# A two-layer hybrid encoder step on one core: bias rows copied in DRAM in three parts, planner costs and stage biases changed

## The chip, the core and the metric

The program runs on one core of a Trainium2 chip. The metric is device microseconds of one execution. The engines are TensorE (PE; its weight loads are shown as PEld), VectorE (DVE), ScalarE (ACT), GpSimdE (POOL) and SyncE (SP). Each runs its own instruction list in order and waits on semaphores for the others. All DMAs of this kernel are issued from SP's list.

## The reference

One inference step of two layers over 576 tokens: 512 prompt tokens and 64 sample tokens with 1024 cached keys. Each layer normalizes x and projects it, and three mixers read the projection:

```python
z = rmsnorm(x, norm_g) @ w_in                  # 1024 -> all columns of A, B, C and the gates
# A: differential attention, 4 heads, two softmax maps per head, T5 bias
bias = bias_a[t5_bucket(k_pos[None, :] - q_pos[:, None])]
logits = q k^T / 8 + bias;  a = p[:, :, 0] - lam * p[:, :, 1];  o = a v
# B: an indexer scores the keys, the top k (128 prompt, 256 sample) are kept, 8 heads attend to them
score = sum_h wi_h * relu(qi_h ki^T);  idx = top_k(score);  logits = q k_sel^T / 8 + bias_b
# C: chunked retention, 4 heads, decay, rotary
y = x + (sum_n sigmoid(gate_n) * ((o_n * silu(g_n)) @ w_branch[n])) @ w_out
```

The T5 bias depends on the distance of key and query alone, for 12 heads (4 of A, 8 of B). Outputs are y, the new keys and values, and the retention states, for prompt and sample.

## The kernel before, in words

Tokens lie in five tiles: t = 0 to 3 of 128 prompt tokens, t = 4 of 64 sample tokens. Every large product is made of three fp32r products of a high and a low part: the weights come by DMA into `wraw` (two buffers), ACT casts them to `whi`, DVE subtracts to `wlo` (two buffers), and PE multiplies hi·hi, lo·hi, hi·lo (`proj_tok`, L622, with tokens in the rows; `proj_ch`, L634, with channels in the rows). `x_norm` (L541 to L565) loads x, normalizes it (DVE, POOL for the power) and transposes it on PE (L562) into `xh` and `xl`.

`wload_idx` and `idx_proj` (L508 to L513, L748 to L755) make the indexer's product first; from it come the keys of B, written out (L737) and transposed by PE (L690). `keys_T` (L669, L670) loads cached keys with four DMAs and transposes them on DVE. `idx_prompt` and `idx_sample` score the keys (L789 to L797), and `topk` finds the largest by rounds of MAX8 and MATCH_REPLACE8 on DVE (L829, L830): 16 rounds for each of three prompt tiles and 32 for the sample, in each layer.

The bias: `build_windows` (L424 to L436, step `w0`) multiplies `rel_bias` by a table of one-hot columns on PE (L431), copies the result to SBUF (L433), writes 12 rows of 352 numbers to `gdram` in DRAM (L435), and copies each row 128 times within DRAM into `grep` (L436; 2112 KB). `dwin` (L438) and `dwin_s` then read skewed windows out of `grep` (L441, L449), into four buffers `D` and one `Ds`, and DVE overwrites a corner of each (L442).

The order of the instructions is not that of the code. A step list (`STEPS`) names the stages (x, i, iq, cv, gc, ...), each with two numbers, one for each layer, its bias in priority. `Order.plan` lists all instructions, gives each a cost (`_cost`), plays the five queues forward in time, and whenever an engine is free takes the ready instruction with the smallest priority (place in the program plus bias). `pin` then ties each engine's instructions into that order. A change of a cost or a bias therefore moves instructions on every engine, and never what they compute.

Of the kernel before, what the change touches and what calls it, by code (L numbers as in the profile page):

```python
# [12 lines left out]
F32 = mybir.dt.float32  # L13
# [74 lines left out]
        "sg": 2, "o": 2, "z": 4, "D": 4, "Ds": 1, "ss": 13, "ssn": 4, "nm": 7, "Z": 3, "sso": 2, "m8": 11, "z3": 1,  # L88
        "zz": 7, "qs": 1, "zk": 1, "qks": 3, "qd": 1}
STEPS = """  # L90
pw0+-2700/-3200 x0+0/-3900 x1+-11000/0 x2+3500/1700 x3+3900 w0+300/-5700 x4+-7800/0 i0+9200/4200 iq0+9300/5200
cv0+9700/1000 i1+-20100/-32500 gc1+-5800/1600 cq0+-800/14000 gc0+15200/18400 ca0+700 cv1+20500/-1900
sc0+3400/4900 cq1+-5100/900 ca1+-3800/-4000 kc0+4200/-400 ak0+2000/1900 i2+-18000/-17000 top2+30200/7600
ga0+0/-4400 sc1+-900 aq0+9200/-800 av0+400/3200 mc3+1200/8900 mc2+11900/-4200 top3+300/13700 aa1+2900/-5300
aa0+1500/-4000 mc0+24100/-3300 vc0+6000/5400 ak1+1400/-100 mc1+-1300/-2800 aq1+-13900/8000 av1+10300/10100
ga1+-8100/-6800 sa0+500/2600 aa3+-5200/-9000 gb0+-500/-6500 top1+0/6200 aa2+-16000/-18400 gb1 top4+30600/28400
kc1+-5500/-9000 bq0+4700/1500 sa1+-5800/-2400 bp0+-5900 ma1+10900/10500 bs0+-19100/-19900 ma0+11500/-2900
bq1+-400/0 bp1 sb0+-4800/-3100 ma3 ma2+5900/5600 bs1+1000/0 sb1+-2300/-5100 mb1+6200 mb0+-1200/-5200 mb2+0/-100
mb3
"""  # L100
PB = {"pj": 3, "s": 2, "t": 3}

# [1 line left out]
class Order:  # L104
# [44 lines left out]
    def _area(self, o):  # L149
# [17 lines left out]
            m = r  # L167
        return t.name, p0, p0 + o.ap[0][1], m << off

    def _cost(self, i, e, ins, outs):  # L170
        cols = self._cols
        n = max(cols(o) for o in ins[:1] + outs[:1]) if ins else cols(outs[0])
        if e == "SP":
            for o in outs[:1]:
                n = cols(o) * o.ap[0][1]
            return n / 90.0
        if e == "PE":
            n = cols(outs[0])
            if outs[0].bass_ap.tensor.name in self.psum and outs[0].bass_ap.offset >= 64 * 512:
                return 94.0  # L180
            if "float32r" in str(ins[0].dtype):
                return max(n * 0.4375 + 7, 112.0)
            if i.is_transpose:
                return 110.0
            return 2 * max(n / 1.2 + 5, 112.0)
        ps = any(o.bass_ap.tensor.name in self.psum for o in ins)
        if e == "Activation":
            return (51 if ps else 94) + n / 1.2 + 93 * (len(outs) - 1) + 93 * (len(ins) > 1)
        if e == "Pool":
            return 300 + 164 * n if "pow" in str(getattr(i, "op", "")) else 145 + n * 2.12  # L190
        op = str(i.opcode)
        if op == "Memset":
            return 40 + n * 0.26
        wide = [o for o in ins if cols(o) > 1]
        fast = not ps and len(wide) == 1 and op in ("TensorCopy", "TensorScalarPtr")
        ptr = op in ("TensorScalarPtr", "ISA") and len(ins) > len(wide) and n > 4
        return 68 + n * (0.52 if fast else 1.042) + 61 * ptr
# [48 lines left out]
    def plan(self):  # L246
        ops, users = self._graph()
        n = len(ops)
# [47 lines left out]
        for _ in range(n):  # L296
# [14 lines left out]
            order[e].append(k)  # L311
            start[k] = t
            if e == "SP":
                clock[e] = t + 475
                dma = max(dma, t + 1100) + cost
                end[k] = dma + 750
            else:
                if e == "PE":
                    if shared != rows:
                        cost += 90 if shared else 190  # L320
                        rows = shared
                    idle = max(0.0, idle + max(0.0, t - clock[e]) - (t - seen) * 0.35)
                    seen = t
                    if idle > 1300 and clock[e] > 0:
                        slow, idle = t + 3400, 0.0
                    if t < slow:
                        cost *= 2
                elif shared:
                    if e == "DVE" and port["Pool"] > t:
                        start[k] = port["Pool"] + 150  # L330
                    elif e == "Pool":
                        start[k] = max(t, port["DVE"])
                clock[e] = end[k] = start[k] + cost
                if shared and e in port:
                    port[e] = end[k]
# [34 lines left out]
def trunk(ctx: ExitStack, tc: tile.TileContext, xp, xs_in, ca_k, ca_v, cb_k, cb_v, cb_ki, st_c, rel_bias,  # L370
# [47 lines left out]
    PS = [sb(256, "Ps") for _ in range(2)]  # L418
    for p in PS:
        nc.gpsimd.memset(p[:, 192:], 0.0)  # L420
    grep = dram.tile([12, 128, 352], F32, name="grep")
    yscr = dram.tile([NTOK, DM], F32, name="yscr")

    def build_windows():  # L424
        oh = sb(512, "P")
        nc.vector.memset(oh[:32, 351:352], 0.0)
        dma(oh[:32, :351], cst[:32, C_OH:C_OH + 351])
        rb = sb(12, "rb")
        dma(rb[:32], rel_bias)
        gps = pb("t")  # L430
        mm(gps[:12, :352], rb[:32], oh[:32, :352], start=True, stop=True)  # L431
        gsb = sb(512, "P")
        nc.vector.tensor_copy(gsb[:12, :352], gps[:12, :352])  # L433
        gdram = dram.tile([12, 352], F32, name="gdram")
        dma(gdram, gsb[:12, :352])  # L435
        dma(grep, bass.AP(tensor=gdram.tensor, offset=gdram.offset, ap=[[352, 12], [0, 128], [1, 352]]))  # L436

    def dwin(h):  # L438
        d = sb(224, "D")
        a = grep[h]  # L440
        dma(d, bass.AP(tensor=a.tensor, offset=a.offset + 127, ap=[[351, 128], [1, 224]]))  # L441
        nc.vector.memset(d[0:64, 160:224], -NEG)  # L442
        return d

    def dwin_s(h0, h1):
        d = sb(160, "Ds")
        for i, h in enumerate((h0, h1)):
            a = grep[h]
            dma(d[64 * i:64 * i + 64],  # L449
                bass.AP(tensor=a.tensor, offset=a.offset + 127, ap=[[351, 64], [1, 160]]))  # L450
        return d
# [68 lines left out]
    for l in range(depth):  # L520
# [772 lines left out]
        def run(step):  # L1293
# [4 lines left out]
                    dma(cs[:, C_COS:], cst[:, C_COS:C_RES])  # L1298
            elif op == "w":
                build_windows() if l == 0 else None  # L1300
            elif op == "pw":
                ready["w"] = wload_idx(l, tt if l == 0 else ptt)
            elif op == "vc":
                vcache()
            elif op == "i":
                (idx_proj, idx_prompt, idx_sample)[arg]()
            elif op == "iq":
                idx_q()
            elif op == "kc":
                KT["ip"[arg]] = kcache_T((cb_ki, cb_k)[arg][l, 0])  # L1310
            elif op == "top":
                topk(arg)
            elif op[0] == "g":
                gates(op[1], {"a": O_AG, "b": O_BG, "c": O_CG}[op[1]], arg)
            elif op[0] == "s":
                split(op[1], arg)
            elif op[0] == "m":
                branch(op[1], arg)
            elif op in ("aq", "ak"):
                a_qk(arg, "qk".index(op[1]))  # L1320
            else:
                {"av": a_val, "aa": a_att, "cv": c_val, "cq": c_qk, "ca": c_att, "bq": b_proj, "bp": b_prompt,
                 "bs": b_sample}[op](arg)
# [68 lines left out]
```

## Time and profile before

| | |
|---|---|
| three runs | 1442.31, 1445.65, 1449.87 us; median 1445.65 us |
| the profiled execution | 1446.73 us |
| its span, from the first to the last instruction | 1444.9 us |
| busy: PE, DVE, ACT, POOL | 1385.6, 1146.3, 663.8, 246.9 us |
| moved by DMA | 127.51 MB, mean 88 GB/s |
| chain of waits that ended last | PE 64%, DVE 20%, ACT 6%, DMA 5% |

[...] A timeline lists one engine's instructions in order; the bracket at a row's end is the idle time just before it and what ended it. Matmuls overlap in the pipeline, so the sum of their durations is above the time between their starts.

### The profile page before, as it was taken

How to read it: one execution, taken by the hardware profiler on the slowest of the kernel's cores; microseconds unless marked ns; L12 is line 12 of the kernel's file. 1: busy time of each engine (PE TensorE's matmuls, PEld its weight loads, DVE VectorE, ACT ScalarE, POOL GpSimd, SP SyncE). 2: the span in 40 equal slices, each digit the busy share in tenths (PEclk: the TensorE clock that was granted, in tenths of full speed). 3: DMA queues.
4: the chain of work that ended last, by engine and by line, in shares of the span. 5: the costliest groups of instructions: out<-in, count | busy, mean ns of one | idle time of the engine just before them, and what ended most of it. 6: DMA issues, size and time to landing. Idle time of an engine off the chain costs nothing.

```text
span 1444.9 us, 27676 instructions
## 1 busy us (share of the span) xinstructions
PE 1385.6 (96%) x10422; PEld 1328.2 (92%) x10422; DVE 1146.3 (79%) x2791; ACT 663.8 (46%) x1631; POOL 246.9 (17%) x294
## 2 busy tenths in 40 slices
PE   5999999999999999999999999999999999999999
PEld 4899989998999989999989998899989998999999
DVE  5799999998776888844487999999997678886433
ACT  5433464445555464433353335543546454644321
POOL 1121432112223020000030333410321120300000
PEclk9999999999999999999999999999999999999999
DMA  7423225222332222324532222232424322121333
GB/s 220 111 73 86 54 72 141 73 76 86 95 94 61 87 59 59 89 67 115 172 103 64 70 74 77 79 100 70 112 65 114 78 68 61 47 73 47 99 122 115
DMA packets 189738, 127.51 MB, mean 88 GB/s; under 512 B 65976, under 2 KB 188388, under 8 KB 189604
## 3 DMA queue, kind: packets, MB, share of 16 engines
q1 hardware_dynamic: 189604, 125.74, 31.1%
q8 instruction: 82, 1.34, 0.4%
q14 instruction: 52, 0.43, 0.1%
HBM read 114.84 MB, written 13.03 MB: 88 GB/s over the span
## 4 chain that ended last, share of the span: by engine, by line
PE 64%; DVE 20%; ACT 6%; DMA 5%; issue 3%; SPq 1%; POOL 1%; DVEq 0%; ACTq 0%
PE pj L634 29%; PE pj L622 11%; PE pj L1352 6%; DVE wlo L496 4%; DVE u L830 3%; DMA wraw<-in_w_in_dram 3%; DVE m L829 3%; PE s L1181 1%; PE t L1193 1%; ACT whi L495 1%; DVE s L468 1%; PE s L998 1%; DVE u L956 1%; PE t L1013 1%; PE t L1045 1%
## 5 line engine op out<-in xcount | busy, mean ns | idle before, releaser
L495 ACT CAST whi<-wraw 128x1024 fp32r<-128x1024 f32 x164 | 172.0, 1049 | 186.6 <-DMA wraw<-in_w_in_dram 73.3
L496 DVE TENSOR_TENSOR wlo<-wraw,whi 128x1024 fp32r<-128x1024 f32 x164 | 199.3, 1226 | 64.7 <-PE pj L634 53.0
L634 PE MATMUL pj<-xh,whi 128*128 128x288 f32 x1216 | 205.9, 299 | 5.3 <-ACT sg L1265 1.9
L634 PE MATMUL pj<-xh,wlo 128*128 128x288 f32 x1216 | 199.8, 297 | 3.9 <-DVE wlo L496 3.9
L634 PE MATMUL pj<-xl,whi 128*128 128x288 f32 x1216 | 200.4, 297 | 0.0
L634 PEld LDWEIGHTS pj<-xh,whi 128*128 128x128 f32 x1216 | 175.0, 188 | 9.1 <-ACT sg L1265 2.3
L634 PEld LDWEIGHTS pj<-xh,wlo 128*128 128x128 f32 x1216 | 173.4, 188 | 7.0 <-DVE wlo L496 5.6
L634 PEld LDWEIGHTS pj<-xl,whi 128*128 128x128 f32 x1216 | 174.1, 188 | 1.2 <-issue 0.3
L829 DVE MAX8 m<-u 64x8 f32<-64x1088 f32 (+3 forms) x160 | 134.9, 845 | 1.7
L830 DVE MATCH_REPLACE8 u<-m,u 64x1088 f32<-64x1088 f32 (+3 forms) x160 | 133.1, 832 | 0.1
L622 PE MATMUL pj<-wlo,xh 128*128 128x256 f32 x768 | 121.5, 289 | 6.5 <-DVE wlo L496 6.4
L455 POOL TENSOR_TENSOR ssn<-ssn,mh 128x4 f32<-128x4 f32 (+1 forms) x70 | 73.2, 1048 | 318.6 <-DVE ssn L454 313.1
L634 PE MATMUL pj<-u,whi 128*128 128x288 f32 x768 | 126.1, 297 | 0.0
L622 PE MATMUL pj<-whi,xh 128*128 128x256 f32 x768 | 117.8, 287 | 3.6 <-ACT whi L495 2.4
L622 PE MATMUL pj<-whi,xl 128*128 128x256 f32 x768 | 115.2, 285 | 0.0
L622 PEld LDWEIGHTS pj<-wlo,xh 128*128 128x128 f32 x768 | 103.1, 191 | 10.0 <-DVE wlo L496 8.5
L634 PEld LDWEIGHTS pj<-u,whi 128*128 128x128 f32 x768 | 110.1, 188 | 0.7
L622 PEld LDWEIGHTS pj<-whi,xh 128*128 128x128 f32 x768 | 102.2, 190 | 6.5 <-ACT whi L495 3.7
L622 PEld LDWEIGHTS pj<-whi,xl 128*128 128x128 f32 x768 | 101.7, 191 | 0.4
L1265 ACT ACTIVATE sg<-pj 128x288 f32<-128x288 f32 x96 | 39.2, 410 | 77.9 <-PE pj L634 77.1
L634 PE MATMUL pj<-u,wlo 128*128 128x288 f32 x384 | 70.5, 299 | 1.2 <-DVE wlo L496 1.2
L1352 PE MATMUL pj<-whi,u 128*128 128x256 f32 x512 | 68.8, 282 | 0.4 <-ACT u L1287 0.4
(280 smaller groups left out, 2547.1 us busy)
## 6 DMA issues: line engine op xcount, KB each, us to landing
wraw<-in_w_in_dram SPq DMA_DIRECT2D x116, 512.0 KB, 3.8
wraw<-in_w_branch_dram SPq DMA_DIRECT2D x24, 512.0 KB, 4.7
wraw<-in_w_out_dram SPq DMA_DIRECT2D x16, 512.0 KB, 4.7
wraw<-in_w_in_dram SPq DMA_DIRECT2D x20, 256.0 KB, 3.4
r<-in_cache_a_k_dram SPq DMA_DIRECT2D x64, 64.0 KB, 2.3
r<-in_cache_a_v_dram SPq DMA_DIRECT2D x16, 256.0 KB, 2.9
out_dram<-u SPq DMA_DIRECT2D x32, 128.0 KB, 2.1
D<-grep SPq DMA_DIRECT2D x24, 112.0 KB, 2.0
```

Source lines behind the costliest of these rows:

```text
L455: ptt(ss, ss, mh[:ss.shape[0], :1].to_broadcast(list(ss.shape)), op=OP.pow)
L468: nc.vector.tensor_tensor_reduce(s, s, d, 1.0, init, OP.add, OP.min, out)
L495: nc.scalar.copy(hi[:, :n], raw[:, :n])
L496: tt(lo[:, :n], raw[:, :n], hi.bitcast(F32)[:, :n], op=OP.subtract)
L622: mm(ps[:M, :ncol], a[:, k, q], b[:, k, :ncol], start=(i == 0 and k == 0), stop=(i == 2 and k == 7))
L634: mm(ps[:, :288], a[:, k, c], b[:, k, q], start=(i == 0 and k == 0), stop=(i == 2 and k == kt - 1))
L829: nc.vector.max(m8[:rows], sc)
L830: nc.vector.match_replace(sc, m8[:rows], sc, SENT)
L956: tt(W_[2 + c][r] if which else w[x], tv[r], w.bitcast(F32)[r], op=OP.subtract)
L998: mm(s[:, :w], Q[c][:, hh, tq], K[c + 2 * i][:, hh, :w], start=i == 0, stop=i == 1)
L1265: lambda q, ps: act(sg[:, q], ps, AF.Tanh, scale=0.5))
L1352: mm(ps[:M, :256], src[:, c0:c0 + M], (hv, hv, lv)[i][:, k], start=(i == 0 and k == 0), stop=(i == 2 and k == 7))
```

## The change

The copy within DRAM leaves `build_windows`. A new step `wg` issues it in three parts, each of 4 heads into a tensor of its own, and `dwin` and `dwin_s` read from the tensor of their head. In the step list, `wg0` stands after `top2`, `wg1` and `wg2` after `mc2`, with biases of their own. The planner's cost of a DMA was bytes in one fixed rate; it is now counted by contiguous runs, with a rate of its own for the copies within DRAM, and SP's issue costs 500 ns instead of 475. TensorE's costs rise by one to two percent (fp32r: 0.4475 ns a column instead of 0.4375, at least 114 ns instead of 112). All biases are new numbers. The diff, cut:

```diff
@@ the table of biases, its first line of before and of now
-pw0+-2700/-3200 x0+0/-3900 x1+-11000/0 x2+3500/1700 x3+3900 w0+300/-5700 x4+-7800/0 i0+9200/4200 iq0+9300/5200
+pw0+0/-28300 x0+-5500/-9500 x1+-4600/-23100 x2+600/1700 x3+-900/-6600 w0+13400/10200 x4+1300/-6900 i0+2200/9800
...
+    @staticmethod
+    def _run(o):
+        n = 1
+        for s, k in reversed(list(o.ap)):
+            if k > 1 and s != n:
+                break
+            n *= k
+        return n
@@ in _cost
         if e == "SP":
-            for o in outs[:1]:
-                n = cols(o) * o.ap[0][1]
-            return n / 90.0
+            n = cols(outs[0]) * outs[0].ap[0][1]
+            run = min(self._run(o) for o in ins[:1] + outs[:1])
+            if all(o.bass_ap.tensor.name.startswith("g") for o in ins[:1] + outs[:1]):
+                return cols(outs[0]) * outs[0].ap[0][1] / 49.0
+            return n / run * max(36.0, run / 6.0) / 16
         if e == "PE":
...
-            if "float32r" in str(ins[0].dtype):
-                return max(n * 0.4375 + 7, 112.0)
+            if fast:
+                return max(n * 0.4475 + 7, 114.0)
             if i.is_transpose:
-                return 110.0
-            return 2 * max(n / 1.2 + 5, 112.0)
+                return 112.0
+            return 2 * max(n / 1.18 + 5, 114.0)
@@ in plan
             if e == "SP":
-                clock[e] = t + 475
+                clock[e] = t + 500
@@ in trunk
-    grep = dram.tile([12, 128, 352], F32, name="grep")
+    gdram = dram.tile([12, 352], F32, name="gdram")
+    grep = [dram.tile([4, 128, 352], F32, name=f"grep{g}") for g in range(3)]
...
-        gdram = dram.tile([12, 352], F32, name="gdram")
         dma(gdram, gsb[:12, :352])
-        dma(grep, bass.AP(tensor=gdram.tensor, offset=gdram.offset, ap=[[352, 12], [0, 128], [1, 352]]))
+
+    def spread_windows(g):
+        dma(grep[g], bass.AP(tensor=gdram.tensor, offset=gdram.offset + 4 * 352 * g,
+                             ap=[[352, 4], [0, 128], [1, 352]]))
@@ in dwin and dwin_s
-        a = grep[h]
+        a = grep[h // 4][h % 4]
@@ in run
+            elif op == "wg":
+                spread_windows(arg) if l == 0 else None
```

**Place 1: the start.** SP's list in the kernel before, from its first row; `wraw` are the indexer's weights, `u` are tiles of x, `cs` constants, `P` the row of norm gains:

```order
L508 DMA wraw_113<-in_w_in_dram 128x4x128
L508 DMA wraw_113<-in_w_in_dram 128x4x68
L508 DMA wraw_122<-in_w_in_dram 128x4x128
L508 DMA wraw_122<-in_w_in_dram 128x4x68
L411 DMA u_63<-in_x_prompt_dram 128x512
L541 DMA u_64<-in_x_prompt_dram 128x1024
L411 DMA u_63<-in_x_prompt_dram 128x512
L413 DMA cs_70<-in_consts_dram 128x192
L1298 DMA cs_70<-in_consts_dram 128x332
L533 DMA P_82<-in_norm_g_dram 128x512
L533 DMA P_83<-in_norm_g_dram 128x512
```

SP's list now, from its first row:

```order
L423 DMA u_63<-in_x_prompt_dram 128x512
L556 DMA u_64<-in_x_prompt_dram 128x1024
L423 DMA u_63<-in_x_prompt_dram 128x512
L425 DMA cs_70<-in_consts_dram 128x192
L548 DMA P_85<-in_norm_g_dram 128x512
L548 DMA P_86<-in_norm_g_dram 128x512
L587 DMA gqka_89<-in_a_qk_g_dram 128x128
L588 DMA gqkb_90<-in_b_qk_g_dram 128x128
L592 DMA gcol_95<-in_a_subln_g_dram 128x1
L593 DMA gcol_95<-in_c_gn_g_dram 128x1
L598 DMA z_100<-in_a_lambda_dram 128x256
L523 DMA wraw_116<-in_w_in_dram 128x4x128
```

x and the norm gains moved ahead of the indexer's four weight loads, which are now 12th to 15th. PE's list in the kernel before, from its first row (`s` are transposes of x, `t_235` is the product for the bias rows, `pj` the indexer's product):

```order
L562 MATMUL s_140<-cs_70,u_63 128x128 x4
L431 MATMUL t_235<-P_230,rb_233 12x352
L562 MATMUL s_148<-cs_70,u_63 128x128 x4
L748 MATMUL pj_272<-whi_116,xh_80 128x392
L562 MATMUL s_165<-cs_70,u_64 128x128 x4
```

PE's list now:

```order
L577 MATMUL s_143<-cs_70,u_63 128x128 x4
L577 MATMUL s_151<-cs_70,u_63 128x128 x4
L577 MATMUL s_168<-cs_70,u_64 128x128 x4
L577 MATMUL s_176<-cs_70,u_64 128x128 x4
L763 MATMUL pj_273<-whi_119,xh_83 128x392 x2
L763 MATMUL pj_317<-whi_119,xh_83 128x392 x2
```

The product for the bias rows left the second place (it now stands inside the indexer's third token tile), and both halves of x tiles 0 and 1 are transposed before the indexer begins.

**Place 2: the copy in SP's list.** In the kernel before (`gdram` are the bias rows, `grep` their copy, `r` cached keys of the indexer):

```order
L493 DMA wraw_493<-in_w_in_dram 128x4x256
L435 DMA gdram<-P_237 12x352
L669 DMA r_1917<-in_cache_b_kidx_dram 32x16x32 x2
L436 DMA grep<-gdram 1536x1x352
L669 DMA r_1917<-in_cache_b_kidx_dram 32x16x32 x2
L737 DMA out_dram<-z_289 128x64 x3
L441 DMA D_3165<-grep 128x224
```

Now, 22 issues later in the list, after all eight loads of those keys:

```order
L508 DMA wraw_634<-in_w_in_dram 128x4x256
L684 DMA r_3177<-in_cache_a_k_dram 32x16x32
L450 DMA grep_79<-gdram 512x1x352
L450 DMA grep_81<-gdram 512x1x352
L752 DMA out_dram<-z_461 64x64
L752 DMA out_dram<-z_422 128x64
L450 DMA grep_80<-gdram 512x1x352
L684 DMA r_3177<-in_cache_a_k_dram 32x16x32 x3
L508 DMA wraw_835<-in_w_in_dram 128x4x256
L456 DMA D_3169<-grep_79 128x224
```

The copy no longer stands between the two halves of a load of keys; its three parts stand within five rows of each other.

**Place 3: layer 1 on DVE, the low halves for the gate of C.** In the kernel before; `m` are the results of the rounds, the first of the layer is `m_11248` and each next one counts up by 3:

```order
L829 MAX m_11251<-u_9790 128x8
L830 MATCH_REPLACE u_9790<-m_11251,u_9790 128x384
L496 TENSOR_TENSOR wlo_9862<-wraw_9860,whi_9861 128x1024
L601 TENSOR_TENSOR pj_9769<-pj_9769,z_9786 64x256
L496 TENSOR_TENSOR wlo_9868<-wraw_9866,whi_9867 128x1024
```

Now, where the first round is `m_11252`:

```order
L844 MAX m_11270<-u_9794 128x8
L511 TENSOR_TENSOR wlo_9866<-wraw_9864,whi_9865 128x1024
L845 MATCH_REPLACE u_9794<-m_11270,u_9794 128x384
L844 MAX m_11273<-u_9794 128x8
L845 MATCH_REPLACE u_9794<-m_11273,u_9794 128x384
L844 MAX m_11276<-u_9794 128x8
L845 MATCH_REPLACE u_9794<-m_11276,u_9794 128x384
L844 MAX m_11279<-u_9794 128x8
L511 TENSOR_TENSOR wlo_9872<-wraw_9870,whi_9871 128x1024
```

The same two low halves stand behind 2 and 2 rounds before, and behind 7 and 10 now.

## Rows read from the trace of the kernel before

**Rows 1.** The page, part 1: busy microseconds, share of the span, instructions.

```profile
PE 1385.6 (96%) x10422; PEld 1328.2 (92%) x10422; DVE 1146.3 (79%) x2791; ACT 663.8 (46%) x1631; POOL 246.9 (17%) x294
```

**Rows 2.** Stretches: length, then busy microseconds of each engine, clock, DMA.

```profile
0.00:20.00 20.00, 5.75 (x19) 4.13 (x20) 9.25 (x32) 8.63 (x22) 2.43 (x11) 1.00 0.86 242
20.00:40.00 20.00, 17.28 (x117) 15.70 (x117) 16.08 (x59) 11.86 (x36) 4.56 (x8) 1.00 0.63 185
40.00:60.00 20.00, 18.26 (x135) 17.38 (x135) 13.20 (x37) 10.12 (x32) 4.22 (x7) 1.00 0.65 155
...
100.00:150.00 50.00, 49.43 (x392) 46.94 (x392) 48.29 (x123) 16.75 (x39) 14.59 (x22) 1.00 0.29 77
...
760.00:780.00 20.00, 18.63 (x135) 17.51 (x134) 11.58 (x25) 7.84 (x17) 0.00 (x0) 1.00 0.23 63
...
800.00:850.00 50.00, 48.57 (x384) 45.80 (x383) 49.07 (x125) 17.13 (x40) 14.14 (x20) 1.00 0.21 60
```

**Rows 3.** Timeline of DVE in layer 1: start, length, instruction, [idle before].

```profile
764.27 1.22 DVE L496 TENSOR_TENSOR wlo<-wraw,whi 128x1024 fp32r<-128x1024 f32 x1 [3.02 <-PE pj L634]
768.68 1.22 DVE L496 TENSOR_TENSOR wlo<-wraw,whi 128x1024 fp32r<-128x1024 f32 x1 [3.19 <-PE pj L634]
...
782.32 1.22 DVE L496 TENSOR_TENSOR wlo<-wraw,whi 128x1024 fp32r<-128x1024 f32 x1
...
784.92 0.55 DVE L829 MAX8 m<-u 128x8 f32<-128x384 f32 x1
...
786.15 0.56 DVE L829 MAX8 m<-u 128x8 f32<-128x384 f32 x1
```

**Rows 4.** Timeline of PE in layer 1, first use of that low half.

```profile
784.11 0.69 PE L634 MATMUL pj<-xh,wlo 128*128 128x288 f32 x4
```

**Rows 5.** Timeline of PE at the start.

```profile
12.54 1.11 PE L562 MATMUL s<-cs,u 128*128 128x128 f32 x4 [12.54 <-DVE u L557]
15.36 1.33 PE L431 MATMUL t<-P,rb 32*12 32x352 f32 x2 [1.71 <-DMA rb<-in_rel_bias_dram]
...
17.39 0.68 PE L748 MATMUL pj<-whi,xh 128*128 128x392 f32 x1
...
19.04 0.85 PE L748 MATMUL pj<-wlo,xh 128*128 128x392 f32 x2
...
23.56 0.52 PE L748 MATMUL pj<-wlo,xh 128*128 128x392 f32 x2
...
37.16 0.33 PE L690 MATMUL t<-cs,zk 128*128 128x128 f32 x1 [2.58 <-DVE zk L459]
...
41.76 0.33 PE L690 MATMUL t<-cs,zk 128*128 128x128 f32 x1 [0.99 <-ACT zk L461]
```

**Rows 6.** Timeline of DVE at the start.

```profile
9.83 0.69 DVE L549 CUSTOM_DVE_ANT_0 r<-u 128x512 f32<-128x512 f32 x1 [1.51 <-DMA u<-in_x_prompt_dram]
...
11.73 2.74 DVE L557 SCALAR_TENSOR_TENSOR u<-u,ss,P 128x512 f32<-128x512 f32 x4 [0.50 <-POOL ss L455]
...
35.89 0.71 DVE L670 STREAM_TRANSPOSE r<-r 128x512 f32<-128x512 f32 x1 [2.71 <-DMA r<-in_cache_b_kidx_dram]
```

**Rows 7.** Timeline of SP's DMA issues at the start.

```profile
0.73 2.09 SPq L508 DMA_DIRECT2D wraw<-in_w_in_dram  x4
2.87 0.50 SPq L411 DMA_DIRECT2D u<-in_x_prompt_dram  x1
...
3.89 0.43 SPq L411 DMA_DIRECT2D u<-in_x_prompt_dram  x1
...
24.34 0.86 SPq L436 DMA_DIRECT2D grep<-gdram  x1
25.25 4.44 SPq L669 DMA_DIRECT2D r<-in_cache_b_kidx_dram  x2
...
35.41 1.75 SPq L441 DMA_DIRECT2D D<-grep  x4
```

**Rows 8.** The instructions of line 829, the search rounds: count, durations in ns, starts.

```profile
L829 DVE MAX8 m<-u x160: 409/687/1289, 65.3 to 1068.7; 64x8 f32<-64x1088 f32 x64, 128x8 f32<-128x384 f32 x32, 128x8 f32<-128x512 f32 x32, 128x8 f32<-128x256 f32 x32
```

More of the change, by code (lines that the diff above doesn't have):

```diff
@@ L90 @@
 STEPS = """
-pw0+-2700/-3200 x0+0/-3900 x1+-11000/0 x2+3500/1700 x3+3900 w0+300/-5700 x4+-7800/0 i0+9200/4200 iq0+9300/5200
[L92 to L99, printed above, removed]
+pw0+0/-28300 x0+-5500/-9500 x1+-4600/-23100 x2+600/1700 x3+-900/-6600 w0+13400/10200 x4+1300/-6900 i0+2200/9800
+iq0+3300 cv0+28300 i1+4700/-10400 gc1+-100/-1600 cq0+1100/5500 gc0+27300/28000 ca0+0/800 cv1 sc0+8400/-100
+cq1+-1200/-33400 ca1+-7800/-6500 kc0+1700/1500 ak0+6600/6400 i2+3500/2600 top2+700/-4200 wg0+-4100/-800
+ga0+-6300/-6800 sc1+1600/900 aq0+-8300/-10800 av0+-2900/-2100 mc3+20400/20000 mc2+33600/6600 wg1+0/600
+wg2+-800/800 top3+0/4600 aa1+8300/9500 aa0+0/-100 mc0+-5800/500 vc0+2900/100 ak1+2100/5200 mc1+-15500
+aq1+-19100/-18100 av1+-12300/-8700 ga1+-8700/-5000 sa0+7000/3800 aa3+-12500/-12100 gb0+300/-4500 top1+8100
+aa2+-1600/-4800 gb1+2400/-3200 top4+54500/56900 kc1+-20300/-4200 bq0+2300/3000 sa1+8800/0 bp0+-400/0
+ma1+33300/2800 bs0+0/3300 ma0+2600/3500 bq1+3300/8400 bp1+-17300 sb0+11700/4500 ma3+12300/12100 ma2+-9100/-6900
+bs1+-44000/-45600 sb1+-8400/-4400 mb1+-1300/-2200 mb0+-1100/-2000 mb2+-1000/-1800 mb3+-200/-800
 """
@@ L173, in _cost @@
         if e == "SP":
-            for o in outs[:1]:
-                n = cols(o) * o.ap[0][1]
-            return n / 90.0
+            n = cols(outs[0]) * outs[0].ap[0][1]
[3 more added lines that the diff above has]
+            return n / run * max(36.0, run / 6.0) / 16
         if e == "PE":
             n = cols(outs[0])
+            fast = "float32r" in str(ins[0].dtype)
             if outs[0].bass_ap.tensor.name in self.psum and outs[0].bass_ap.offset >= 64 * 512:
                 return 94.0
-            if "float32r" in str(ins[0].dtype):
-                return max(n * 0.4375 + 7, 112.0)
+            if fast:
+                return max(n * 0.4475 + 7, 114.0)
             if i.is_transpose:
-                return 110.0
-            return 2 * max(n / 1.2 + 5, 112.0)
+                return 112.0
+            return 2 * max(n / 1.18 + 5, 114.0)
         ps = any(o.bass_ap.tensor.name in self.psum for o in ins)
@@ L447, in dwin_s @@
         for i, h in enumerate((h0, h1)):
-            a = grep[h]
+            a = grep[h // 4][h % 4]
             dma(d[64 * i:64 * i + 64],
```

## The prediction

> **What bounds the kernel now.** I read the engines' totals first, then the stretch table, then the timelines of the stretches that the table shows to be loose. PE is busy for 1385.6 of 1444.9 us [rows 1], so 59.3 us of idle PE is all that a new order could win outright; the work itself does not change. The stretch table says where the idle is: in the first 60 us PE is busy for 5.75 + 17.28 + 18.26 = 41.3 us, so 18.7 us are lost there, and the other 40.6 us are spread over 1385 us, about 3% [rows 2]. The reader is to see two different things. At the start PE waits for the first data. Later, in 100 to 150 and 800 to 850 us, PE and DVE are both above 96% busy [rows 2]: DVE holds the rounds of the top-k search besides the low halves of the weights, and PE gets each low half just before it needs it. In layer 1 one is finished at about 783.5 (782.32 + 1.22) [rows 3] and first used at 784.11 [rows 4], a margin of 0.6 us.
>
> The start itself has three losses. PE's first transposes begin at 12.54 us. Then it waits 1.71 us for the bias table's data, since that product stands second in its list, and the indexer begins at 17.39 [rows 5]. At 37.16 and 41.76 it waits again, 2.58 and 0.99 us, for transposes of keys that DVE and ACT prepare [rows 5]. The cause is on DVE: from 33.2 to 35.89 DVE sits 2.71 us at the transposition of cached keys, waiting for their DMA [rows 6]. Two of the four loads of those keys were issued at 25.25, directly behind the 2112 KB copy issued at 24.34; the copy was done about when the windows could be read, at 35.41 [rows 7], and so were they.
>
> **The change part by part.** The sum is made against the profiled execution's own 1446.73 us (the span and 1.8 us around it); the median of the runs is 1445.65, 1.1 us less.
>
> *The copy leaves the keys' way.* All eight loads of the indexer's keys are now issued ahead of it. DVE's stall goes, and with it PE's 2.58 + 0.99 = 3.57 us [rows 5]. Bounds: 0 if something else on DVE is just as late, 3.57 if nothing is. I take 3.6, because DVE needs no other DMA there and the last load now waits only for the first outputs of the indexer. The three parts are still 2112 KB and stand close together, so the copy does move later but is hardly spread; in 24.34 to 35.41 it took 11.1 us. What is queued behind it on SP are three loads of cached keys for A, a weight load for the gate of C and the windows. The windows are needed only by a corner write on DVE that stands after the first three search rounds. The first round begins at 65.3 us in the old order [rows 8], and I expect the copy over before 50, so I cost it at nothing; if that cover is gone, DVE stops at the corner write and the low halves behind it come late by as much. Two more issues cost SP at most 2 x 0.86 us [rows 7], which nobody waits for.
>
> *The first DMAs.* Without the four weight loads in front, x issues 2.87 - 0.73 = 2.14 us earlier [rows 7]. The second half of tile 0 was issued at 3.89 and DVE began on it at 9.83; from there to its scaling at 11.73 and the transposes at 12.54 are 2.71 us [rows 5 to 7]. With the landing time unchanged it lands at 9.83 - 2.14 = 7.7, and the transposes begin at 10.4. The indexer's first product now needs its weights, 12th in the list instead of first. The bounds come from what must precede it: at best 2.14 + 1.71 us go and another 1 us because less data shares the DMA engines, so it starts at 12.5; at worst only the 1.71 us wait for the bias table goes and it starts at 15.7. I take 13.9, near the middle: transposes from 10.4, four groups at 1.11 us or so each [rows 5], minus the overlap with the weights' casts. That is 17.39 - 13.9 = 3.5 us, within 1.7 and 4.9.
>
> PE runs slowly at first: two products of 392 columns take 0.85 us at 19.04 and 0.52 at 23.56 [rows 5], half and full clock. I let that slow period move forward with the rest and cost it at nothing. [...]
>
> *New biases in the body.* PE passes through the stages in the same sequence as before; what shifts is how they are interleaved, and how many search rounds DVE does ahead of each low half. In layer 0 the count is up by two to four at the second projections of C and back to even at the values of A. Those low halves have no margin, so I charge 1.0 us that is not recovered; bounds 0, since the extra rounds are caught up later, and 2.5, two rounds at 1.23 us [rows 3].
>
> In layer 1 the rounds come forward: 7 and 10 instead of 2 and 2 ahead of the two low halves for the gate of C, and nine more ahead of those for the keys of A. This is paid for from idle time: DVE is busy for only 11.58 us of 760 to 780 [rows 2], and waits 3.02 + 3.19 = 6.2 us there for PE to release a buffer [rows 3]. In the new order PE finishes the indexer's queries before it goes far into the values of C, so the buffers come free sooner. The DVE-bound stretch behind it, up to the last round at 1068.7 us [rows 8], then has up to 6.2 us less to do. PE must keep up, and it has its own 3% of waits. Bounds: -6.2 if all is won, +4 if the rounds ahead cost more than the idle they fill; I take -2.5. The planner's higher PE costs and the DMA costs act only through the order; they have no other price. What is late next, once the head is shorter, is the low halves, in both layers.
>
> Sum: -3.6 - 3.5 + 1.0 - 2.5 = -8.6 us, 1438.1 for an execution like the profiled one; less 1.1 for the median, **1437 us**.
>
> **The rivals.**
>
> *The head's gain is not passed on (no change).* In 100 to 150 us DVE is busy for 48.29 of 50 us [rows 2]. If DVE's own start does not come forward with PE's, PE arrives early and waits at the first low halves. For it: no margin in the low halves. Against: DVE was idle in the first 60 us for 60 - 9.25 - 16.08 - 13.20 = 21.5 us [rows 2], mostly waiting for the same data. Then perhaps 3 us stay: 1446.73 - 3 - 1.1 = 1442.6, range 1439 to 1447.
>
> *Search rounds hold up the low halves (slower).* In layer 1, nine more rounds ahead of the low halves for the keys of A, at 1.23 us each [rows 3], are 11.1 us, against a margin of 0.6 us. If PE does not release the buffers sooner, none of this is hidden, and PE waits for it and does not win it back. With a head gain of only the 3.6 us of the keys, the time is 1446.73 + 11.1 - 3.6 - 1.1 = 1453 us. It decides from the point where the rounds cost 7.2 us more than the head saves. For it: the rounds stand directly in front of those halves. Against: the idle of rows 3, and that the total of rounds is even again by the end of the stretch.
>
> *The body gains more.* If the new biases also take a fifth of the 40.6 us of scattered idle, 8 us more: 1429 us.
>
> **How the numbers follow.** This kernel's measurements tell about 0.5% from no change, 7.2 us: below 1438.4 counts as faster, above 1452.9 as slower. The forecast has 0.55, with its own range 1431 to 1442; four fifths of that lie under 1438.4 or so (0.45), the rest is no change (0.10). The unshared head gain has 0.25, nearly all of it no change. The rounds have 0.13, of which 0.12 are slower. The larger gain has 0.07. So 0.52 faster, 0.36 same, 0.12 slower. The range takes in the first two cases, most of the larger gain and the lower edge of the slow case: 1427 to 1450, with about 0.07 left out below and 0.09 above.
>
> **What would show it.** In the new profile: first transposes near 10.4 us and the indexer's first product near 13.9; no wait of PE of over 1 us between 25 and 45 us; PE busy for some 48 of the first 60 us; DVE not stopped at the corner write of the windows; in layer 1 DVE idle for under 5 us between 750 and 775; the low halves of the keys of A in layer 1 ready at least 7 us earlier than before. It is wrong if the indexer starts later than 15.7 us, if the clock rises later in the work, or if PE's waits for low halves in layer 1 sum to over 6 us.

## The result: 1.1% slower, and the profile after

The changed kernel takes 1462.99 us (median of 4 runs, 1461.25 to 1464.53), the kernel before 1447.69 (4 runs): a ratio of 1.0111, 95% interval [1.0076, 1.0145]. The forecast was 1437 in a range of 1427 to 1450. The page of the new profile, its totals and slices of 36.6 us:

```profile
span 1462.6 us, 27679 instructions
PE 1400.7 (96%) x10422; PEld 1337.3 (91%) x10422; DVE 1153.5 (79%) x2791; ACT 666.7 (46%) x1631; POOL 243.2 (17%) x294
PE   7899999999999999999999999899999999999999
PEclk9899999999999999999999999999999999999999
```

The span is 17.7 us longer than before, and 15.1 of these are busy PE time, with the same 10422 instructions as in [rows 1]: longer waits are not the whole loss. One slice stands out, the second, where the granted clock was also less than full. The stretch table, with the columns of [rows 2] (start and end, length, then for PE, PEld, DVE, ACT and POOL the busy us and the count of instructions, then the clock granted to PE, where 1.00 is the full level, the busy share of the 16 DMA engines, and GB/s):

```profile
0.00:20.00 20.00, 9.89 (x35) 8.46 (x36) 11.77 (x41) 11.83 (x30) 2.51 (x12) 1.00 0.88 259
20.00:40.00 20.00, 19.77 (x140) 18.14 (x139) 16.97 (x60) 11.67 (x39) 5.29 (x12) 1.00 0.41 85
40.00:60.00 20.00, 19.89 (x147) 19.13 (x146) 16.01 (x39) 9.81 (x26) 1.20 (x3) 1.00 0.36 115
60.00:80.00 20.00, 12.88 (x82) 12.52 (x80) 10.56 (x29) 3.62 (x6) 0.00 (x0) 0.74 0.62 172
```

The first 60 us went as forecast: PE busy 49.55 us (48 forecast; 41.3 in [rows 2]). Then comes what the forecast costed at nothing. PE's timeline:

```profile
8.70 1.97 PE L577 MATMUL s<-cs,u 128*128 128x128 f32 x8 [8.70 <-DVE u L572]
...
13.41 1.68 PE L763 MATMUL pj<-whi,xh 128*128 128x392 f32 x4
...
62.79 0.28 PE L628 MATMUL pj<-whi,xh 128*128 128x256 f32 x1
70.18 1.33 PE L649 MATMUL pj<-xh,whi 128*128 128x288 f32 x4 [7.12 <-ACT whi L510]
...
77.34 0.69 PE L649 MATMUL pj<-xh,wlo 128*128 128x288 f32 x4
```

PE stops for 7.12 us, and what follows runs at half clock: four products of 288 columns take 1.33 us at 70.18 and 0.69 at 77.34 (the trace's clock records show the half level from 65.6 to 75.8 us). The cast on ACT that PE waits for waits itself for its weights:

```profile
69.09 1.04 ACT L510 CAST whi<-wraw 128x1024 fp32r<-128x1024 f32 x1 [8.61 <-DMA wraw<-in_w_in_dram]
```

DVE's timeline beside it:

```profile
59.67 0.54 DVE L845 MATCH_REPLACE8 u<-m,u 128x384 f32<-128x384 f32 x1
67.73 0.71 DVE L685 STREAM_TRANSPOSE r<-r 128x512 f32<-128x512 f32 x1 [7.52 <-DMA r<-in_cache_a_k_dram]
...
69.53 0.11 DVE L457 MEMSET D<- 64x64 f32 x1 [0.64 <-DMA D<-grep]
...
73.09 0.11 DVE L457 MEMSET D<- 64x64 f32 x1 [0.88 <-DMA D<-grep]
```

DVE waits 7.52 us for cached keys of A, then for the windows. All of this leads to SP's DMA issues:

```profile
39.26 0.50 SPq L684 DMA_DIRECT2D r<-in_cache_a_k_dram  x1
39.84 4.63 SPq L450 DMA_DIRECT2D grep<-gdram  x2
44.57 7.62 SPq L752 DMA_DIRECT2D out_dram<-z  x2
52.23 0.63 SPq L450 DMA_DIRECT2D grep<-gdram  x1
52.90 10.15 SPq L684 DMA_DIRECT2D r<-in_cache_a_k_dram  x3
63.17 1.76 SPq L508 DMA_DIRECT2D wraw<-in_w_in_dram  x1
64.97 2.71 SPq L456 DMA_DIRECT2D D<-grep  x3
```

Behind the copy's parts (39.84 and 52.23) SP itself is held: three loads of 64 KB take 10.15 us to issue, and the weights that PE misses at 62.79 are issued at 63.17. Why the copy lasts so long stands in the DMA view: busy tenths and GB/s in 40 slices, of the kernel before in 24 to 36 us (0.3 us a slice),

```profile
DMA  0000003677778667787788789788987898999500
GB/s 12 0 0 0 0 0 80 230 253 268 235 249 243 221 221 236 244 280 259 246 284 282 265 295 313 285 307 286 357 297 291 301 323 270 186 164 174 120 18 2
```

and of the changed one in 42 to 67 us (0.6 us a slice):

```profile
DMA  9352222222222222342222222222362463362579
GB/s 222 92 114 95 101 88 95 97 99 97 99 97 95 95 99 97 114 134 97 95 97 95 95 97 91 97 95 99 113 155 97 135 154 101 111 159 91 81 155 336
```

The DMA engines are busy for two tenths and move 97 GB/s, against seven to nine tenths and some 250. By the trace's packet records, the 1536 packets of 1408 bytes take a median of 60 ns each in both kernels. Before they ran from 25.96 to 34.77 us, their times sum to 99.9 us: 11.3 at a time. Now they run from 42.33 to 66.14, sum 96.2 us: 4.0 at a time. Counted moment by moment, the most frequent number under way was 12 before (3.2 of 8.8 us) and is 4 now (16.1 of 23.8 us). The outer dimension of the copy was 12 heads and is 4, like the most frequent numbers of packets under way. The records name no engine: that a copy runs on as many DMA engines as its outer dimension has entries is the author's theory (theory 1 of e1, e2 and e8), and the runs show it in packets under way alone.

### The profile page after: what moved, and what is told of

The parts are those of the page before. It is cut to its first block, busy times and chain, and to the rows that moved or that the text cites. A ratio compares the mean times of both kernels' runs of the same rounds, so it can differ in the third digit from the quotient of the medians.

```text
span 1462.6 us, 27679 instructions
## 1 busy us (share of the span) xinstructions
PE 1400.7 (96%) x10422; PEld 1337.3 (91%) x10422; DVE 1153.5 (79%) x2791; ACT 666.7 (46%) x1631; POOL 243.2 (17%) x294
## 4 chain that ended last, share of the span: by engine, by line
PE 52%; DVE 16%; ACT 5%; DMA 3%; issue 3%; POOL 1%; POOLq 0%; DVEq 0%; ACTq 0%; SPq 0%
PE pj L649 25%; PE pj L637 6%; PE pj L1369 6%; DVE wlo L511 3%; DVE u L845 2%; DMA wraw<-in_w_in_dram 2%; DVE m L844 2%; PE s L1196 1%; PE t L1208 1%; DVE s L483 1%; PE s L1013 1%; ACT whi L510 1%; PE t L1028 1%; DVE P L1179 1%; PE s L1211 1%
## 5 line engine op out<-in xcount | busy, mean ns | idle before, releaser
L511 DVE TENSOR_TENSOR wlo<-wraw,whi 128x1024 fp32r<-128x1024 f32 x164 | 199.6, 1228 | 65.3 <-PE pj L649 55.0
L649 PE MATMUL pj<-xh,whi 128*128 128x288 f32 x1216 | 206.9, 300 | 11.2 <-ACT whi L510 9.5
L649 PE MATMUL pj<-xh,wlo 128*128 128x288 f32 x1216 | 205.7, 299 | 4.0 <-DVE wlo L511 4.0
L649 PE MATMUL pj<-xl,whi 128*128 128x288 f32 x1216 | 197.5, 297 | 0.0
L649 PEld LDWEIGHTS pj<-xh,whi 128*128 128x128 f32 x1216 | 177.0, 190 | 16.2 <-ACT whi L510 10.8
L649 PEld LDWEIGHTS pj<-xh,wlo 128*128 128x128 f32 x1216 | 175.2, 188 | 8.6 <-DVE wlo L511 6.2
L649 PEld LDWEIGHTS pj<-xl,whi 128*128 128x128 f32 x1216 | 173.6, 189 | 0.7
L637 PE MATMUL pj<-whi,xh 128*128 128x256 f32 x768 | 121.0, 288 | 5.3 <-ACT whi L510 4.6
L649 PE MATMUL pj<-u,whi 128*128 128x288 f32 x768 | 125.9, 297 | 0.0
L649 PEld LDWEIGHTS pj<-u,whi 128*128 128x128 f32 x768 | 109.8, 188 | 0.6
L649 PE MATMUL pj<-u,wlo 128*128 128x288 f32 x384 | 70.7, 299 | 0.9 <-DVE wlo L511 0.8
```

Of the source, the lines that this page charges most:

```text
L511: tt(lo[:, :n], raw[:, :n], hi.bitcast(F32)[:, :n], op=OP.subtract)
L637: mm(ps[:M, :ncol], a[:, k, q], b[:, k, :ncol], start=(i == 0 and k == 0), stop=(i == 2 and k == 7))
L649: mm(ps[:, :288], a[:, k, c], b[:, k, q], start=(i == 0 and k == 0), stop=(i == 2 and k == kt - 1))
```

## The experiments

Besides medians, some readings compare PE at equal work: its matmuls in order, each counted with the short time usual for its shape in the kernel before, and the time at which the same sum is reached. In us against the kernel before (minus is ahead), one profiled execution each; another choice of the usual time moves a reading by up to 1 us. Ratios are to executions of the kernel before measured beside each run, whose medians lie between 1446.2 and 1447.6 us.

```
before at       58    79   129   457   763   871  1091  1433
changed       -7.3   2.8   6.2   6.6   9.6  14.3  19.0  17.5
e1            -8.2  -8.0  -4.2  -3.3   0.2   3.6   8.3   7.5
e12           -7.5  -5.0  -5.0  -2.5  -4.0  -4.4  -5.0  -5.6
e13            1.1   2.1   5.8   6.5  10.3  14.9  18.9  18.4
e14           -7.3  -7.0  -3.3  -2.9   2.4   1.9   1.8   1.4
e15           -7.9  -6.5  -6.2  -4.1  -4.5  -1.1   3.4   2.6
```

**e1, the copy with its rows outermost.** Nothing else moves on any engine.

```diff
-        dma(grep[g], bass.AP(tensor=gdram.tensor, offset=gdram.offset + 4 * 352 * g,
-                             ap=[[352, 4], [0, 128], [1, 352]]))
+        dma(bass.AP(tensor=grep[g].tensor, offset=grep[g].offset, ap=[[352, 128], [128 * 352, 4], [1, 352]]),
+            bass.AP(tensor=gdram.tensor, offset=gdram.offset + 4 * 352 * g, ap=[[0, 128], [352, 4], [1, 352]]))
```

> The changed kernel, with one edit: each of the three parts of the copy within DRAM is written with the 128 rows as its outer dimension in place of the 4 heads. Instruction order is the same on every engine. Theory 1 (the parts run on few DMA engines): the 1536 packets of 1408 bytes, 60 ns each, took 42.3 to 66.1 us, which is four of them at a time; on 16 engines at a time they need 1536 x 60 / 16 = 5.8 us, so the copy ends near 50 and DVE's 7.5 us and PE's 7.1 us stops at 60 to 70 us go. PE stands 7.2 us ahead of the kernel before at 58 us and 2.8 us behind it at 79, so 10 us of the loss go at once: 1463 - 10 = 1453 us; if the lag that grows by some 7 us in 90 to 360 us comes from the rounds that DVE lost in its stop, it goes too: 1446 us. Theory 2 (the copy is just issued too late, 39.8 in place of 24.3 us): its rate does not matter, the stops stay, 1460 us or more. Theory 3 (the new biases cost the body, the copy is a side matter): 1458 us or more.

1452.51 us, ratio to before 1.0038 [1.0024, 1.0052]. The copy takes 41.14 to 50.36 us, 12.2 packets at a time and most often 15 or 16. SP's issues and PE at the place of the stop:

```profile
42.86 1.02 SPq L450 DMA_DIRECT2D grep<-gdram  x1
43.92 3.94 SPq L684 DMA_DIRECT2D r<-in_cache_a_k_dram  x3
47.98 1.08 SPq L508 DMA_DIRECT2D wraw<-in_w_in_dram  x1
```

```profile
61.82 0.28 PE L628 MATMUL pj<-whi,xh 128*128 128x256 f32 x1
61.94 0.69 PE L649 MATMUL pj<-xh,whi 128*128 128x288 f32 x4
```

The weights are issued 15.2 us sooner, the stop is gone, and so are about 10 us: 10.5 by the two medians, 9.5 when each is taken against the kernel before measured beside it. Theory 1 holds, as far as packets under way tell the engines, and theory 2 falls: in the same late place the copy no longer stops PE. Theory 3 falls as far as it calls the copy a side matter. Theory 1's hope for another 7 us fails: something in the body (all that follows the start) still loses.

**e8, the split alone, in the old place** (kernel before, heads outermost).

```diff
-        dma(grep, bass.AP(tensor=gdram.tensor, offset=gdram.offset, ap=[[352, 12], [0, 128], [1, 352]]))
+        for g in (0, 4, 8): dma(grep[g:g + 4], bass.AP(tensor=gdram.tensor, offset=gdram.offset + 352 * g, ap=[[352, 4], [0, 128], [1, 352]]))
```

> The kernel before, with its copy cut in three parts of 4 heads in the old place, each with the heads as the outer dimension; old biases and costs. Theory 1 (4 heads as outer dimension means four DMA engines): the 1536 packets take 23 us from about 24 on, in place of 11; the loads of keys behind it land some 12 us later, DVE's wait of 2.7 us becomes about 14 and PE's 3.6 us become 12 to 15: 1446.7 + 10 = 1457 us, more if the clock falls in the gap. Theory 2 (splitting alone costs nothing): 1445 to 1449 us.

1460.77 us, 1.0096 [1.0077, 1.0115]. The copy takes 24.20 to 52.80 us, 3.4 packets at a time. DVE's waits for loads behind it:

```profile
33.95 0.71 DVE L670 STREAM_TRANSPOSE r<-r 128x512 f32<-128x512 f32 x1 [6.79 <-DMA r<-in_cache_b_kidx_dram]
...
43.71 0.71 DVE L670 STREAM_TRANSPOSE r<-r 128x512 f32<-128x512 f32 x1 [5.16 <-DMA r<-in_cache_b_kidx_dram]
...
54.60 0.71 DVE L670 STREAM_TRANSPOSE r<-r 128x512 f32<-128x512 f32 x1 [6.66 <-DMA r<-in_cache_a_k_dram]
```

Splitting by four heads costs 13.8 us by itself (1446.99 beside it); place and biases are as before, and the two more issues move other work only in the first 3% of PE's list. Of the 13.8 us, 10 were forecast, more if the clock fell: it did, to the half level for 6.8 us from 33.5 and again from 53.9.

**e2, the kernel before with the rows outermost** (its copy written as in e1, 12 heads inside).

> The kernel before, its one copy within DRAM written with the 128 rows as the outer dimension in place of the 12 heads; instruction order unchanged. Theory 1: the copy ran on 12 engines (its 1536 packets of 1408 bytes took 24.3 to 35.4 us with other transfers); on 16 it ends a little sooner, at best 1536 x 60 / 16 = 5.8 against 7.7 us, and the keys behind it with it: DVE's wait of 2.71 us shrinks to 1 us or so, and the time by at most 2 us, 1444 to 1448. Rival (the engines are shared with the loads anyway, and the copy is bound by something else): no change in the wait.

1447.95 us, 1.0007 [0.9994, 1.0020]; the copy ends at 31.73. DVE's wait for the keys shrinks to 1.2 us as theory 1 had it, but PE then waits 2.6 us for a cast; the 2 us that it is ahead at 46 us in its trace are gone at 58. No measurable gain.

**e3, e4, e6, e7: biases and costs exchanged.** e3 and e4 put the biases of before (of layer 1; all) into e1, e6 the new costs into the kernel before, e7 the old costs into e1.

> The first edit (copy with 128 rows as outer dimension), and the biases of layer 1 as in the kernel before; those of layer 0 are the new ones. Theory 3 (the new biases of layer 1 cost time: PE falls 8 us further behind between 760 and 1090 us in the changed kernel): 7 to 8 us less than the run with the first edit alone. Rival (the lag of layer 1 only passes on what layer 0 lost, or comes with the planner's new costs): within 2 us of it.

> The first edit, and all biases as in the kernel before except those of the new step for the copy; the new planner costs stay. If the head's gain of 7 us is the work of the new biases, it is lost here; if the body's loss is theirs too, it is gone as well: near the kernel before, 1445 to 1450. If the new planner costs by themselves spoil or mend the order: 1455 or more, or 1440 or less.

> The kernel before, biases, copy and all, with only the planner's costs changed to the new ones (TensorE, DMA and SP's issue). Theory C (biases fit only the costs they were chosen with, by the order that they give): 1460 us or more, as with the old biases under new costs in the run before (1488 us). Rival (the copy's steps, not the costs, spoiled that run): within 5 us of 1447.

> The changed kernel with the copy's parts written rows outermost, and the planner's old costs; the new biases stay. Theory C: the new biases under old costs give a worse order than under the new, 1458 us or more against 1452.5. Rival (the new costs themselves are what spoils the body): 1446 us or less.

1462.29, 1488.41, 1486.51 and 1491.66 us; ratios 1.0105 [1.0089, 1.0121], 1.0282 [1.0264, 1.0300], 1.0278 [1.0257, 1.0298] and 1.0318 [1.0294, 1.0341]. Theory C holds: old biases under the new costs take 41.7 and 39.5 us more than the kernel before beside them (e4, e6), new biases under the old costs 39.2 more than e1 (e7). The mix of the two sets (e3) takes 9.8 more than e1, where theory 3 forecast 7 to 8 less. So none of these runs says what the new order costs, and theory 3 is not tested by them. For that the order itself has to be carried over.

**e9, e5, e10: only the start.** e9 moves the copy of the kernel before two rows down in SP's list. e5 takes four biases of layer 0; e10 also moves the copy behind all eight loads of keys, and four corner writes to just ahead of the first round.

```diff
-pw0+-2700/-3200 x0+0/-3900 x1+-11000/0 x2+3500/1700 x3+3900 w0+300/-5700 x4+-7800/0 i0+9200/4200
+pw0+0/-3200 x0+-5500/-3900 x1+-4600/0 x2+3500/1700 x3+3900 w0+13400/-5700 x4+-7800/0 i0+9200/4200
```

> The kernel before, with only its copy moved in SP's list: two rows later, behind the first four loads of the indexer's keys (it stood between the second and the third). Everything else as before, 12 heads outermost. Theory A (the keys' wait is worth what PE waits at it, and the body passes it on): DVE's wait of 2.71 us and PE's of 2.58 go, 1447 - 2.5 = 1444.5 us. Theory B (another transfer, or the second four loads, is just as late): within 1 us of 1447.

> The kernel before with its one copy written rows outermost, and four new biases of layer 0 alone (0 for the index weights, -5500 and -4600 for x0 and x1, 13400 for w0): the start is reordered as in the changed kernel (x ahead of the index weights, the bias product off the second place on PE), and behind the first 130 rows of PE's and DVE's lists nothing moves. Theory A (the head's gain reaches the end when the body keeps its order, and the changed kernel lost it to the body's new order): PE is 5 to 8 us ahead at 58 us and keeps it; 1446.7 - 6 = 1441 us. Theory B (the body is bound by DVE or otherwise gives back what the head wins): 1445 to 1448 us.

> The run with the reordered start alone, with its copy (rows outermost) moved behind all eight loads of the indexer's keys, and the first four corner writes of the windows put just ahead of the first search round on DVE. Body order as in the kernel before. Theory A (a gain of the head reaches the end when the body keeps its order): DVE's wait of 4.6 us and PE's of 4.3 at 37.8 us go; PE is 5 to 8 us ahead at 58 us and keeps it: 1441 us. Theory B (the body gives the head's gain back): 1445 to 1448 us.

1446.53, 1447.55 and 1448.70 us; ratios 0.9998 [0.9988, 1.0009], 1.0000 [0.9986, 1.0015] and 1.0010 [0.9997, 1.0023]. e9 lies where its theory B put it, within 1 us of before, though its trace has PE 1.8 us ahead at 58 us. e5 and e10 do not test theory A, since neither has its gain at 58 us: PE is 0.4 us ahead there, and 2.0 behind. One load takes the place of another. DVE in e5, and in e10:

```profile
36.96 0.71 DVE L670 STREAM_TRANSPOSE r<-r 128x512 f32<-128x512 f32 x1 [4.57 <-DMA r<-in_cache_b_kidx_dram]
```

```profile
45.56 0.71 DVE L681 STREAM_TRANSPOSE r<-r 128x512 f32<-128x512 f32 x1 [3.03 <-DMA r<-in_cache_a_k_dram]
```

**e11, the halves ahead of the rounds** (e1, with a move in DVE's list).

```diff
+        v, r = order["DVE"], ("Max", "MatchReplace", "MatchValueLoad")
+        for j in range(len(v)):
+            if "wlo" in ops[v[j]][0].outs[0].bass_ap.tensor.name:
+                f = j
+                while f > j - 4 and str(ops[v[f - 1]][0].opcode) in r:
+                    f -= 1
+                v.insert(f, v.pop(j))
```

> The changed kernel with the copy's parts written rows outermost, and on DVE each low half moved ahead of up to two search rounds that stand directly in front of it (26 moves, both layers). Theory D (the rounds ahead of the low halves make the body's loss: PE waits 7.2 us for low halves and 4.3 us for high halves in 760 to 1110 us, against 5.4 and 1.1 before): these waits fall to 6 us or less together, 1452.5 - 5 = 1447 us. Rival (the halves' weights or buffers are not there earlier, so DVE only waits): 1452 us or more.

1487.71 us, 1.0284 [1.0271, 1.0298]: 35 us more than e1. What DVE waited for in 760 to 1110 us (total, times, longest), in e11 and in e1 (an edit shifts line numbers: L518 and L656 of e11 are L511 and L649 of e1):

```profile
DVE wlo L518 <- PE pj L656: 15.9, 6, 6.1
DVE wlo L518 <- ACT whi L517: 4.0, 1, 4.0
DVE wlo L518 <- PE pj L637: 3.9, 4, 1.8
```

```profile
DVE wlo L511 <- PE pj L649: 1.3, 2, 1.2
```

The rival holds: the halves could not be made sooner, because PE had not released their buffer, and DVE stood waiting where it had done rounds. Theory D's cure fails; that the rounds cost nothing in e1 is not shown by this.

**e12 to e15: orders carried over.** Both plans are made in one kernel (copy with rows outermost), and each engine's list is cut: in e12 and e13 at the first round's planned start, in e14 and e15 also at PE's first transposes of layer 1. e12, where `cut` is that time, `order` the new plan's lists and `rest` the old plan's:

```diff
+        self.old = 1
+        rest = self.plan()[1]
+        head = {k for o in order.values() for k in o if start[k] < cut}
+        for e in order:
+            order[e] = [k for k in order[e] if k in head] + [k for k in rest[e] if k not in head]
```

> Instruction lists put together from two plans: up to the first search round every engine has the order of the changed kernel (its copy's parts written rows outermost), from there on the order of the kernel before. In the run of the changed kernel with that copy PE stood 8.2 us ahead at 58 us. Theory A (the head's gain reaches the end when the body keeps its old order; the new body order loses some 15 us by itself): 1447 - 7 = 1440 us. Theory B (the old body, bound by DVE and by just-in-time halves, gives the gain back): 1445 to 1448 us.

> The other half of the same pair: up to the first search round the order of the kernel before (with the copy in three parts, rows outermost), from there on the order of the changed kernel. Theory A (the new body order is what loses, whatever the head): 1452.5 + 8 = 1460 us, at least 1455. Theory B (the body's loss in the changed kernel is only its head's gain given back): 1447 to 1450 us.

> Again lists put together from two plans: start and layer 0 in the order of the changed kernel (copy with rows outermost), layer 1 in the order of the kernel before; the cut is at PE's first transposes of layer 1. Against the run with only the start new (1441.0), PE of the changed kernel falls back 3 us in layer 0 and 10 us in layer 1. Theory E (the loss sits where PE falls back, mostly in the order of layer 1): 1444 us. Rival (the order of layer 1 only pays for the state that layer 0 leaves): 1450 us or more.

> The complement: start new, layer 0 behind it in the order of the kernel before, layer 1 in the order of the changed kernel. Theory E: 1441 + 10 = 1451 us. Rival: 1445 us or less.

| | start | layer 0 | layer 1 | us | against before beside it, us | ratio to before |
|---|---|---|---|---|---|---|
| e2 | old | old | old | 1447.95 | +1.2 | 1.0007 [0.9994, 1.0020] |
| e12 | new | old | old | 1441.02 | -5.2 | 0.9965 [0.9955, 0.9975] |
| e14 | new | new | old | 1447.17 | -0.5 | 0.9996 [0.9987, 1.0006] |
| e15 | new | old | new | 1448.93 | +1.3 | 1.0007 [0.9997, 1.0017] |
| e1 | new | new | new | 1452.51 | +5.8 | 1.0038 [1.0024, 1.0052] |
| e13 | old | new | new | 1461.78 | +15.5 | 1.0110 [1.0094, 1.0126] |

Theory A holds: with the old body most of the start's gain reaches the end (5.2 us against before, 6.9 by the medians of e2 and e12), and the new body loses 11.0 us with the new start and 14.3 with the old. e12 is faster than both kernels. Theory E holds by half, since e14 and e15 both lie between its forecasts and the rival's: layer 1 alone loses 6.5 us and layer 0 alone 4.8 (7.9 and 6.2 by the medians), and PE falls back where each order is new: at 763 us e14 stands at 2.4 and e12 at -4.0, and e15 goes from -4.5 there to 3.4 at 1091.

The clock does not explain the body's loss: executions with a mean granted clock of 1.000 took 1452.5 us in e1 (two) and 1439.7 to 1441.9 in e12 (five). What PE waited for in 760 to 1110 us, in e12 and in e15 (L675, L687, L549 and L548 of e12 are L679, L691, L553 and L552 of e15):

```profile
PE pj L675 <- DVE wlo L549: 3.0, 3, 1.4
PE pj L687 <- DVE wlo L549: 2.4, 4, 1.2
...
PE pj L675 <- ACT whi L548: 1.1, 1, 1.1
```

```profile
PE pj L679 <- DVE wlo L553: 4.4, 4, 1.6
PE pj L691 <- DVE wlo L553: 2.8, 5, 1.6
PE pj L679 <- ACT whi L552: 2.8, 3, 1.2
PE pj L691 <- ACT whi L552: 1.5, 2, 0.8
```

Halves of weights: 6.5 us of waits with the old order of layer 1, 11.5 with the new. Other waits shrink, so idle PE grows by 3.8 us in this window, from 12.5 to 16.3. The rest of the loss is no idle time at all. PE's totals in e12, e14, e15 and e1, whose spans are 1439.5, 1446.5, 1447.7 and 1452.5 us:

```profile
PE 1385.2 (96%) x10422; PEld 1328.3 (92%) x10422; DVE 1146.2 (80%) x2791; ACT 664.8 (46%) x1631; POOL 244.6 (17%) x294
PE 1390.7 (96%) x10422; PEld 1329.3 (92%) x10422; DVE 1147.7 (79%) x2791; ACT 665.8 (46%) x1631; POOL 244.4 (17%) x294
PE 1389.0 (96%) x10422; PEld 1328.0 (92%) x10422; DVE 1150.8 (79%) x2791; ACT 665.0 (46%) x1631; POOL 242.7 (17%) x294
PE 1396.9 (96%) x10422; PEld 1333.7 (92%) x10422; DVE 1153.4 (79%) x2791; ACT 667.1 (46%) x1631; POOL 242.8 (17%) x294
```

From e12 to e1 the span grows by 13.0 us, PE's busy time by 11.7. In e14 and e15, with a granted clock of 1.000 as in e12, the busy time grows by 5.5 and 3.8 us. Why the same products keep PE busy longer in the new order was not traced.

## Why the prediction was wrong

**The start: right.** Forecast 3.6 + 3.5 = 7.1 us; PE is 7.3 ahead at 58 us, and with the old body 5.2 to 6.9 reach the end. Transposes begin at 8.70 (10.4 forecast), the indexer at 13.41 (13.9), and no wait over 1 us stands between 25 and 45. The 1 us that a lighter load of the DMA engines was to win at best was an estimate that no run shows: in the first 20 us they were busy for 0.88, and for 0.86 before [rows 2]. The two terms are not separate, as the sum had them: e9, e5 and e10, with a part of the edit each, gain nothing measurable.

**The step that failed: "I expect the copy over before 50, so I cost it at nothing".** It took the 11.1 us of the old copy (from its issue to the windows'; its packets took 8.8) for the three parts, on "the three parts are still 2112 KB". The bytes are the same, but their outer dimension fell from 12 to 4, and with it the packets in flight from 11.3 to 4.0: 23.8 us, until 66.1. The prediction listed the three loads of keys and the weight load that stand behind the copy on SP, but asked only when the windows were needed; these loads were hit first. "Two more issues cost SP at most 2 x 0.86 us" failed with it: the parts held SP for 4.63 and 0.63 us and the loads behind them for 10.15. Price: about 10 us (e1). The planner made the same mistake: it prices a copy at one nanosecond for 49 elements, so three parts of 180224 cost 11.03 us, about what the old, 12-wide copy took from its issue to the windows', and the order was made with that.

**The body: wrong in sign.** Forecast 1.0 - 2.5 = -1.5 us; measured +11.0 (e1 against e12, each against before). The step behind both terms was that the order acts through waits alone: "59.3 us of idle PE is all that a new order could win outright; the work itself does not change". Idle PE changed by 1.3 us from e12 to e1, busy PE by 11.7. The rival of search rounds in layer 1, with 0.13, named 11.1 us; that this is near the whole body's loss is luck, since layer 1 lost 6.5 to 7.9 of it and layer 0 the rest, and e11 does not bear out its mechanism: moving halves ahead of rounds made DVE wait for their buffer. Two of the prediction's own signs fell here: in 750 to 775 us DVE idles for 7.4 us (under 5 expected), and PE's waits for low halves in 760 to 1110 sum to 7.2 us (over 6 was to mean wrong). The cause inside the body stays open beyond the 3.8 us of waits. The count of rounds ahead of each half, on which the term was built, says little without the time at which the buffer is free.

**The head's gain not passed on: wrong.** e12 passes on 5.2 us or more of 7.3, though PE and DVE are both above 96% busy in 100 to 150 us [rows 2].

**The clock.** The clock column reads 1.00 in the first 20 us of both tables, but the trace's clock records begin only at 21.9 us in the kernel before and at 21.2 in the changed one, with the full level. Until then PE runs as at the half level: in the changed kernel the indexer's products of 392 columns start 0.327 us apart at 13.9 and 0.179 apart at 23.28, and at the recorded half level those of 288 columns start 0.240 us apart at 70.8, so 0.83 ns a column in both places. The sum let the slow period move forward with the rest at no cost, and a clock that rises later in the work was to mean wrong. It does by a little: 40 matmuls, transposes included, had run by then, 27 before. e1, with the same lists there, has the full clock at 19.1 and is 0.9 us further ahead at 58; so the start's part is about that. The larger price was after the stop: 12.88 busy us in 60 to 80, at a mean granted clock of 0.74.

The steps from e2 to e12 (start, -6.9 us), to e1 (body, +11.5) and to the changed kernel (copy, +10.5) add up to the measured 1463.0 by construction. What supports each is a second reading: against before, the start gains 5.2 us; with the old start, the body loses 14.3; and the copy costs 10.0 by PE's lag at the end (17.5 against 7.5) and 13.8 in the old place (e8).

In the prediction's chances, "four fifths" of 1431 to 1442 under 1438.4 does not come out of an even spread, which gives two thirds.

## What to carry to other kernels

A split that kept the bytes changed the copy's rate here: the packets of its 2112 KB took 8.8 us with 12 heads outermost, 23.8 with 4 and 9.2 with 128 rows (e1). So look at the outermost dimension before pricing a copy by an old duration, and try the rows outermost. What stood behind the slow copy on the queue paid too: SP took 10.15 us to issue three loads of 64 KB, and the weights behind them were issued 15.2 us later than in e1. Biases found under one cost model cost 39 to 42 us here under the other, so to learn what a new order costs, carry the order over piece by piece (two starts by two bodies) instead of mixing its parameters.

## What was not expected of the hardware

- SP was held behind the slow copy: three loads of 64 KB took it 10.15 us to issue with the copy at 4.0 packets at a time, and 3.94 in e1 with the copy at 12.2.
- Rows outermost in place of 12 heads brought less than in place of 4: 11.3 to 13.5 packets at a time in the kernel before, and no time gained (e2), against 4.0 to 12.2 and about 10 us (e1).
- Seven microseconds of idle PE cost ten: it stood 7.3 us ahead before the stop and 2.8 behind at 79, since the clock stayed at half level for 5.6 us of the work that followed (70.2 to 75.8).
